# Two of three pairs of the layers' networks by seven block products, and modulation rows in the token mixings

## The chip, the cores and the metric

The kernel runs on one core of one Trainium2 chip, as one program. The metric is its device time in microseconds (us): the median of three runs of the kernel before was 2988.95 us (2986.76 to 2989.94). The engines are TensorE (PE, with its weight load PEld), VectorE (DVE), ScalarE (ACT), GpSimd (POOL) and SyncE (SP), whose queue issues nearly all transfers from device memory.

## The reference

A model of two blocks runs on one sequence of 512 tokens of width 1024. The first block has two layers, each a token mixing and a gated network with a convolution over the tokens; the second block has two swiglu networks with a bidirectional mLSTM and pooling mixer between them. All is float32. Vectors c, c_2 and c_ctx_2 are turned into modulation columns (shifts, scales and gates) by products with large matrices.

```
def first_block(x, c, ...):
    c_act = silu(c)
    for l in range(2):
        mod = (c_act @ ada_w[l] + ada_b[l])[:, None, :]           # 6 x 1024
        sh1, sc1, g1, sh2, sc2, g2 = split(mod, 6)
        h = rmsnorm(x, norm1_g[l]) * (1 + sc1) + sh1
        x = x + g1 * token_mix(h, w_in[l], w_fourier[l], w_ret[l], w_out[l])
        h = rmsnorm(x, norm2_g[l]) * (1 + sc2) + sh2
        x = x + g2 * conv_ffn(h, ffn_up[l], conv_w[l], conv_b[l], ffn_down[l])
    return rmsnorm(x, final_g)

def conv_ffn(h, w_up, conv_w, conv_b, w_down):                    # 1024 -> 2 x 2816 -> 1024
    u = h @ w_up
    up = pad(u, one token on each side)
    u = sum(up[:, i:i + S] * conv_w[i] for i in range(3)) + conv_b
    a, b = split(u, 2)
    return (gelu(a) * b) @ w_down

def second_block(x, c, ctx, c_ctx, w_mod, ...):
    mod  = (silu(c) @ w_mod + b_mod)                              # 9 x 1024, for x
    modc = (silu(c_ctx) @ w_mod + b_mod)                          # for the 256 context tokens
    # swiglu(x) and swiglu(ctx), mLSTM and pooling mixer, swiglu(x); each with ada_in, ada_out
```

token_mix projects h to seven parts, mixes one by a Fourier transform and three by chunked retention, merges the two results by sigmoid gates and projects them out.

## The kernel before

Activations lie with features on the 128 partitions and tokens along the columns. Every float32 operand is kept as a high and a low part, and a product is three matmuls: high by high, low by high, high by low (`mm`, lines 143 to 155). A weight block is loaded by `wload` (line 109): a transfer to one of four raw buffers, the high part by ACT (line 123), the low part by DVE (line 124). The network of a layer (`ffn`, line 383) runs over 22 pairs of 128 gate and 128 value columns. An ordinary pair is two weight blocks of 1024 × 128 times 512 tokens: 2 × 8 × 3 = 48 matmuls of 512 columns. Behind every group of five or six pairs stands a down projection. In the layers, the pair's two results go through the convolution (ACT line 854, DVE lines 855 and 857, each half), the gelu (ACT) and its product (DVE line 1054), and are split for the down projection (lines 140 and 141).

A pair can also be computed as a quad: its two 1024 × 128 blocks are seen as 2 × 2 blocks of 512, the activations as 2 × 2 blocks of 256 tokens by 512 features, and seven block products take the place of eight. `quad_w` (line 327) makes the sums and differences of weight blocks on DVE and splits them (lines 334 to 341); `combos` (line 302) makes four sums of activation blocks once per network, and splits them; `quad` (line 346) runs the seven products, 7 × 4 × 3 = 84 matmuls of 256 columns, and puts them together with ACT and DVE (lines 363 to 376). The kernel before does this in the networks of the second block, from pair 5 on.

The modulation columns are made by rows: a 512 KB load into a raw buffer and one multiplication with an accumulated sum on DVE (`modcols`, lines 259 to 272). They are a background: every `wload` adds a rate to a counter, and whenever the counter is over one the next row is issued. `drain_bg` issues what is left. In the first token mixing 32 rows are made so (rate 0.6), in the first network the 48 rows of layer 1 (0.8), in the second token mixing 32 rows of the second block (0.5), in the second network the other 40 blocks, each for two vectors (0.68). Which instruction stands behind which on an engine is fixed when the program is built, by a scheduler that starts from the program's order.

The profiled kernel's stages are: first token mixing to 545 us, first network to 925, second token mixing to 1420, second network to 1800, first swiglu network to 2320, mixer to 2607, last swiglu network from 2640 to the end.

Of the kernel before, what the change touches and what calls it, by code (L numbers as in the profile page):

```python
# [19 lines left out]
P = 128  # L20
D = 1024
KD = D // P
S = 512
# [19 lines left out]
    ("n1g", DEPTH * 8), ("n2g", DEPTH * 8), ("adab", DEPTH * 48), ("fing", 8),  # L43
    ("convw", DEPTH * 3 * 44), ("convb", DEPTH * 44),
    ("bmod", 72), ("npre", 24), ("npost", 24),
    ("convw2", 12), ("convb2", 4), ("pscale", 4), ("hnorm", 4),
]
COFF = {}
_o = 0
for _n, _c in COLS:  # L50
    COFF[_n] = _o
    _o += _c
NCOLS = _o


@with_exitstack
def tile_two_blocks(ctx: ExitStack, tc: tile.TileContext, I, out):
# [43 lines left out]
    def col(name, i):  # L101
        o = COFF[name] + i
        return cols[:, o:o + 1]

# [241 lines left out]
    def quad(w, B, tc_, n, mid=None):  # L346
# [10 lines left out]
        if 2 * n <= S:  # L357
            t, u2 = T(), T()[:, n:2 * n]
            s1, u3 = t[:, 0:n], t[:, n:2 * n]
        else:  # L360
            s1, u2, u3 = (T()[:, :n] for _ in range(3))
# [21 lines left out]
    def ffn(segs, up, down, groups, act_fn, sink, fp, bufs, heads, tails, hold=True,  # L383
# [59 lines left out]

        ready = {}

        def quad_prep(j):
            ready[j] = quad_w([up[j], up[NPAIR + j]])

        for at, (kind, gi, j) in enumerate(order):

            coming = None
            if seven and at + 1 < len(order) and order[at + 1][0] == "p" and order[at + 1][2] >= nh + 2:
                coming = lambda j=order[at + 1][2]: quad_prep(j)
            if kind == "p" and seven and nh <= j < nh + 2:
                seven["sums"](j - nh)
            if kind == "p" and seven and j == nh + 2 and "third" in seven:
                seven["third"]()
            if kind == "p" and seven and j >= nh + 2:
                hl, hid[j] = hid_slots(seven["last"] if j == NPAIR - 1 and "last" in seven else None)
                seven["fn"](*quad(ready.pop(j), seven["B"], seven["T"], seven["n"], coming), hl)  # L460
                if j == NPAIR - 1:
                    seven["end"]()
# [88 lines left out]
    ada = {i: ada_load(i) for i in (8, 0)}  # L551
    cols = cst.tile([P, NCOLS], F32, name="cols")
    sp.dma_start(cols, I["cols"])
    mods = []
# [6 lines left out]
    def mod1(l, idx, raws=None):  # L561
        modcols(I["adaT"][l], [(crow, mods[l][0], 48)], idx, raws)
# [11 lines left out]
    def token_mix(l, h, after, before_tail, ws, mo, mp, mid=None):  # L574
# [133 lines left out]
        with tc.tile_pool(name=f"fou{l}", bufs=1) as fp:  # L708
# [77 lines left out]
            seq(ps[:16], [[t.rearrange("p g k -> p (g k)") for t in asp[st]] for st in (0, 1)], tabs[0])  # L786
            Pt.append(split_bias(ps[:16], first[:16, 0:1], 16))

        with tc.tile_pool(name=f"mrg{l}", bufs=1) as gp:
# [70 lines left out]

    c2rows = []
    m2r = cst.tile([P, 2, 72], F32, name="m2r")
# [3 lines left out]

    def mod2(i):
        if not c2rows:
            c2rows.append(silu_row(I["c2"], crp))
        if i < 40 and len(c2rows) < 2:  # L870
            c2rows.append(silu_row(I["cc"], hq["pool"]))
        modcols(I["wmodT"], [(c2rows[0], m2r[:, 0, :], 72)] + ([(c2rows[1], m2r[:, 1, :], 40)] if i < 40 else []), [i])

# [124 lines left out]
    for l in range(DEPTH):  # L998
# [3 lines left out]
        if l == 0:  # L1002
            start0(mp)
            for i in range(16, 24):
                bgq.append(lambda i=i: mod1(0, [i]))
            bgq.append(lambda: fin1(0, 16, 24))
            for i in range(24, 48):
                bgq.append(lambda i=i: mod1(0, [i]))
            bgq.append(lambda: fin1(0, 24, 48))
            bgr[1] = 0.6  # L1010
        else:
            for i in range(40, 72):
                bgq.append(lambda i=i: mod2(i))
            bgr[1] = 0.5
        h = hq["h"]
# [16 lines left out]
        def start_ffn():  # L1032
            if l == 0:
                for i in range(48):
                    bgq.append(lambda i=i: mod1(1, [i]))
                bgq.append(lambda: fin1(1, 0, 48))
            else:
                for i in range(40):
                    bgq.append(lambda i=i: mod2(i))
            bgr[1] = 0.8 if l == 0 else 0.68  # L1040

        def before_ffn_tail():
            drain_bg(0.0)
# [12 lines left out]

        def sink1(si, m, ps, c, first):
# [14 lines left out]
        with tc.tile_pool(name=f"ffn{l}", bufs=1) as fp:  # L1072
            hq["pool"] = fp
# [23 lines left out]

    def swiglu_quad(pa, c12, c21, c22, hl):
        n = hl[0].shape[1] // 2
        one = 2 * n <= S  # L1100
        s_ = T() if one else None
        for i, (g, v) in enumerate(((pa, c21), (c12, c22))):
            t = s_[:, i * n:(i + 1) * n] if one else T()[:, :n]
            act.activation(t, g, AF.Sigmoid)
            dve.tensor_tensor(t, t, g, op=ALU.mult)
            if not one:
                dve.tensor_tensor(t, t, v, op=ALU.mult)
                split(t, *(a[:, i * n:(i + 1) * n] for a in hl))
        if one:
            dve.tensor_tensor(s_, s_, c21, op=ALU.mult)  # L1110
            split(s_, *hl)

# [51 lines left out]
    with tc.tile_pool(name="ffa", bufs=1) as fp:  # L1164
# [28 lines left out]
        def reload():  # L1193
            xc[:] = xc_load(xc_tile())
            x[:] = x_cols(x_tile())
            for k in range(KD):
# [6 lines left out]
            seven={"sums": sums, "third": lambda: third(B, Ts, N3), "B": B, "T": Ts, "n": N3,  # L1203
                   "fn": swiglu_quad, "end": lambda: None,
                   "last": [tz[:, i * T2:(i + 1) * T2] for i in (0, 1)]})
# [321 lines left out]
    with tc.tile_pool(name="ffb", bufs=1) as fp:  # L1527
        qs = ExitStack()
        qps = []

        def slot2():
            if not qps:
                qps.append(qs.enter_context(tc.tile_pool(name="qq", bufs=1, side="right")))
            return [qps[0].tile([P, 256], F32R, name=nm("tc")) for _ in (0, 1)]

        Ts2 = [[], [], [], []]
        B2 = [mcols(hlast[4 * i:4 * i + 4], c) for i in (0, 1) for c in HALVES]
        ffn([(S, hlast)], I["up2T"][1], I["down2T"][1], GROUPS3, swiglu, sink2([z]), fp, 8,
            (3, [(0, c) for c in HALVES]), [(0, c, finish) for c in HALVES], ws=headw,
            seven={"sums": lambda i: combos(B2, slot2, Ts2, (2 * i, 2 * i + 1), 256), "B": B2, "T": Ts2, "n": 256,  # L1540
                   "fn": swiglu_quad, "end": qs.close})

# [114 lines left out]
```

## Time and profile before

| | |
|---|---|
| median of three runs | 2988.95 us |
| the profiled run, its span | 2986.76 us, 2985.0 us |
| PE busy | 2919.9 us, 98% |
| DVE busy | 2115.3 us, 71% |
| ACT busy | 1155.5 us, 39% |
| mean rate of the transfers | 117 GB/s |
| mean granted PE clock | 0.990 |

The span goes from the first to the last instruction; the run's time is a little longer. Busy times are those of one profiled execution, and an engine can be busy without setting the end. [...] In a timeline a row is: start, duration, engine, line, operation, output and inputs, and in square brackets the idle time before it and what ended it. Where DVE or PE works back to back, the next instruction starts a little before the one ahead has ended, so a duration is longer than the distance to the next start. In a list of waits a row is: engine, its line, who released it, total us, times, longest.

### The profile page before, as it was taken

How to read it: one execution, taken by the hardware profiler on the slowest of the kernel's cores; microseconds unless marked ns; L12 is line 12 of the kernel's file. 1: busy time of each engine (PE TensorE's matmuls, PEld its weight loads, DVE VectorE, ACT ScalarE, POOL GpSimd, SP SyncE). 2: the span in 40 equal slices, each digit the busy share in tenths (PEclk: the TensorE clock that was granted, in tenths of full speed). 3: DMA queues.
4: the chain of work that ended last, by engine and by line, in shares of the span. 5: the costliest groups of instructions: out<-in, count | busy, mean ns of one | idle time of the engine just before them, and what ended most of it. 6: DMA issues, size and time to landing. Idle time of an engine off the chain costs nothing.

```text
span 2985.0 us, 42346 instructions
## 1 busy us (share of the span) xinstructions
PE 2919.9 (98%) x16612; PEld 2574.6 (86%) x16612; DVE 2115.3 (71%) x3756; ACT 1155.5 (39%) x1994; POOL 174.1 (6%) x121
## 2 busy tenths in 40 slices
PE   6999999999999999999999999999999999899998
PEld 4888888988889888888888899999999987789997
DVE  8766455777766665556888868677776677686786
ACT  4333333433343333334433345333233456444342
POOL 2000001000000000001000010000000180200001
PEclk9999999999999999999999999999999999999999
DMA  6444354266552333344355532122123220313331
GB/s 250 124 129 130 97 156 142 92 190 191 185 168 90 121 105 115 119 143 148 109 179 179 171 111 86 57 68 74 57 75 110 85 71 15 99 44 112 101 114 57
DMA packets 117560, 348.39 MB, mean 117 GB/s; under 512 B 12432, under 2 KB 26384, under 8 KB 117360
## 3 DMA queue, kind: packets, MB, share of 16 engines
q1 hardware_dynamic: 116208, 344.64, 36.6%
q8 instruction: 130, 2.13, 0.3%
q10 hardware_dynamic: 1152, 1.05, 0.1%
q14 instruction: 70, 0.57, 0.1%
HBM read 341.44 MB, written 4.19 MB: 116 GB/s over the span
## 4 chain that ended last, share of the span: by engine, by line
PE 93%; DVE 4%; ACT 1%; issue 0%; DMA 0%; POOL 0%; SPq 0%; DVEq 0%; ACTq 0%; POOLq 0%
PE mm L151 28%; PE mm L154 28%; PE mm L152 28%; PE sm L185 2%; PE mm L1454 1%; PE mm L626 1%; PE mm L628 1%; PE mm L627 1%; PE sm L193 1%; PE mm L1435 1%; PE mm L1249 0%; PE mm L1250 0%; DVE acc L225 0%; PE mm L1251 0%; DVE hl L242 0%
## 5 line engine op out<-in xcount | busy, mean ns | idle before, releaser
L123 ACT ACTIVATE whi<-raw 128x1024 fp32r<-128x1024 f32 (+3 forms) x467 | 449.8, 965 | 768.5 <-PE mm L152 500.5
L151 PE MATMUL mm<-hh,whi 128*128 128x512 f32 (+2 forms) x1988 | 730.4, 369 | 6.9 <-ACT hh L987 5.3
L152 PE MATMUL mm<-hl,whi 128*128 128x512 f32 (+2 forms) x1988 | 728.4, 367 | 2.5 <-DVE hl L242 2.2
L154 PE MATMUL mm<-hh,wlo 128*128 128x512 f32 (+2 forms) x1988 | 729.1, 367 | 1.4 <-POOL wlo L124 1.4
L124 DVE TENSOR_TENSOR wlo<-raw,whi 128x1024 fp32r<-128x1024 f32 (+4 forms) x450 | 499.0, 1115 | 248.6 <-ACT whi L123 244.3
L151 PEld LDWEIGHTS mm<-hh,whi 128*128 128x128 f32 x1988 | 376.2, 190 | 68.7 <-ACT hh L987 6.2
L152 PEld LDWEIGHTS mm<-hl,whi 128*128 128x128 f32 x1988 | 376.8, 190 | 61.9 <-DVE hl L242 3.0
L154 PEld LDWEIGHTS mm<-hh,wlo 128*128 128x128 f32 x1988 | 376.6, 190 | 59.1 <-POOL wlo L124 2.1
L151 PE MATMUL mm<-dh,whi 128*128 128x512 f32 (+1 forms) x760 | 275.0, 362 | 0.0
L152 PE MATMUL mm<-dh,whi 128*128 128x512 f32 (+1 forms) x760 | 268.4, 361 | 0.0
L154 PE MATMUL mm<-dh,wlo 128*128 128x512 f32 (+1 forms) x760 | 251.7, 362 | 0.0
L271 DVE SCALAR_TENSOR_TENSOR t<-ada,crow 128x1024 bf16<-128x1024 f32 x202 | 244.7, 1216 | 4.7 <-DMA ada<-adaT 4.7
L151 PEld LDWEIGHTS mm<-dh,whi 128*128 128x128 f32 x760 | 143.1, 188 | 29.3
L152 PEld LDWEIGHTS mm<-dh,whi 128*128 128x128 f32 x760 | 142.9, 188 | 23.2
L154 PEld LDWEIGHTS mm<-dh,wlo 128*128 128x128 f32 x760 | 133.1, 188 | 16.7
L124 POOL TENSOR_TENSOR wlo<-raw,whi 128x1024 fp32r<-128x1024 f32 x17 | 42.0, 2499 | 1760.8 <-ACT whi L123 1759.1
L855 DVE SCALAR_TENSOR_TENSOR t<-mm,cols,t 128x511 f32<-128x511 f32 (+1 forms) x96 | 70.6, 735 | 73.6 <-ACT t L854 73.2
L151 PE MATMUL mm<-tc,whi 128*128 128x256 f32 (+1 forms) x386 | 113.2, 295 | 0.0
L154 PE MATMUL mm<-tc,wlo 128*128 128x256 f32 (+1 forms) x386 | 112.4, 292 | 0.0
L152 PE MATMUL mm<-tc,whi 128*128 128x256 f32 (+1 forms) x368 | 106.6, 290 | 0.0
L1119 DVE TENSOR_TENSOR z<-z,mm 128x512 f32<-128x512 f32 (+1 forms) x112 | 67.3, 607 | 55.0 <-PE mm L154 54.6
L854 ACT ACTIVATE t<-mm,cols 128x512 f32<-128x512 f32 (+1 forms) x96 | 72.8, 759 | 70.8 <-PE mm L154 70.6
(478 smaller groups left out, 5871.8 us busy)
## 6 DMA issues: line engine op xcount, KB each, us to landing
ada<-adaT SPq DMA_DIRECT2D x96, 512.0 KB
raw<-winT SPq DMA_DIRECT2D x96, 512.0 KB
raw<-upT SPq DMA_DIRECT2D x88, 512.0 KB
raw<-up2T SPq DMA_DIRECT2D x88, 512.0 KB
ada<-wmodT SPq DMA_DIRECT2D x72, 512.0 KB
raw<-downT SPq DMA_DIRECT2D x32, 384.0 KB
raw<-down2T SPq DMA_DIRECT2D x22, 512.0 KB
raw<-downT SPq DMA_DIRECT2D x32, 320.0 KB
```

Of the source, the lines that this page charges most:

```text
L123: act.activation(hi[:p, :n], raw, AF.Copy)
L124: (eng or dve).tensor_tensor(lo[:p, :n], raw, f(hi[:p, :n]), op=ALU.subtract)
L151: pe.matmul(ps, lhsT=wh, rhs=r[k][0], start=first and k == 0, stop=False, skip_group_check=more)
L152: pe.matmul(ps, lhsT=wh, rhs=r[k][1], start=False, stop=False, skip_group_check=more)
L154: pe.matmul(ps, lhsT=wl, rhs=r[k][0], start=False, stop=last and k == n - 1, skip_group_check=more)
L185: pe.matmul(pm[:, t:t + 1], lhsT=sq[:, t * P:(t + 1) * P], rhs=meanc[:, mc:mc + 1], start=False, stop=i == len(parts) - 1 and t == nt - 1)
L193: pe.matmul(pr[:, t * P:(t + 1) * P], lhsT=y[:, t:t + 1].to_broadcast([P, P]), rhs=identL, start=True, stop=True)
L271: dve.scalar_tensor_tensor(junk, raw[:, :D], 1.0, vec, op0=ALU.mult, op1=ALU.mult, accum_out=dst[:, i:i + 1])
L626: pe.matmul(ps, lhsT=hh, rhs=wh, start=k == 0, stop=False)
L854: act.activation(t, ps, AF.Identity, bias=col(bname, bi), scale=col(wname, taps[1] + wi))
L855: dve.scalar_tensor_tensor(t[:, 1:n], ps[:, 0:n - 1], col(wname, taps[0] + wi), t[:, 1:n], op0=ALU.mult, op1=ALU.add)
L1119: dve.tensor_tensor(zz, zz, ps, op=ALU.add)
```

## The change

In the networks of the two layers, pairs 5, 6, 8, 9, 11, 12, 14, 15, 17, 18 and 20 become quads; the others from 3 on (3, 4, 7, 10, 13, 16, 19, 21) stay ordinary. The sums of activations are made at pairs 3 and 4. The convolution of a quad reads its results from SBUF; ACT copies one of its four blocks there. The frame for quads of 512 tokens becomes a helper, `seven512`, used in the layers and in the last network. The 48 rows of layer 1 move from the first network to the first token mixing (rate 1.28), and the rows of the second network to the second token mixing (rate 1.68), where the context's 40 rows load their blocks by themselves. The networks have no background of rows any more. The constants of the convolution (352 of 632 columns) are loaded at each layer network's start and no longer in the kernel's opening. The first swiglu network's quad function is separated from the last one's.

```
+NCOLS1 = COFF["convw"]
-        return cols[:, o:o + 1]
+        return cols[:, o:o + 1] if o < NCOLS1 else hq["ccols"][:, o - NCOLS1:o - NCOLS1 + 1]
...
+    def seven512(h, fn, **more):
+        qs = ExitStack()
+        qps = []
...
+        Ts = [[], [], [], []]
+        B = [mcols(h[4 * i:4 * i + 4], c) for i in (0, 1) for c in HALVES]
+        return {"sums": lambda i: combos(B, slot, Ts, (2 * i, 2 * i + 1), 256), "B": B, "T": Ts, "n": 256,
+                "fn": fn, "end": qs.close, **more}
...
+        nq = [j for j in range(nh + 2, NPAIR) if seven and seven.get("only", lambda j: True)(j)]
...
-            if kind == "p" and seven and j >= nh + 2:
+            if kind == "p" and j in nq:
...
-    def mod2(i):
...
+    def mod2(i, w_):
+        if w_ not in c2rows:
+            c2rows[w_] = silu_row(I["cc"], hq["pool"]) if w_ else silu_row(I["c2"], crp)
+        modcols(I["wmodT"], [(c2rows[w_], m2r[:, w_, :], 72)], [i])
...
-            bgr[1] = 0.6
+            for i in range(48):
+                bgq.append(lambda i=i: mod1(1, [i]))
+            bgq.append(lambda: fin1(1, 0, 48))
+            bgr[1] = 1.28
         else:
-            for i in range(40, 72):
-                bgq.append(lambda i=i: mod2(i))
-            bgr[1] = 0.5
...
+            for i in range(40):
+                bgq.append(lambda i=i: mod2(i, 1))
+            for i in range(72):
+                bgq.append(lambda i=i: mod2(i, 0))
+            bgr[1] = 1.68
...
         def start_ffn():
-            if l == 0:
-                for i in range(48):
-                    bgq.append(lambda i=i: mod1(1, [i]))
...
-            bgr[1] = 0.8 if l == 0 else 0.68
+            pass
...
+        def geglu_quad(j, hl, pa, v, t):
+            act.activation(v[:, 0:256], pa, AF.Copy)
+            split(geglu(v, t, j, S), *hl)
...
+            hq["ccols"] = fp.tile([P, NCOLS - NCOLS1], F32, name=nm("ccols"))
+            sp.dma_start(hq["ccols"], I["cols"][:, NCOLS1:])
...
-                      before_tail=before_ffn_tail, mid=mid, defer=True)
+                      before_tail=before_ffn_tail, mid=mid, defer=True,
+                      seven=seven512(h, geglu_quad, only=lambda j: j % 3 != 1 and j < NPAIR - 1))
```

On PE, in the first network, pair 4 (outputs mm_5270 and mm_5271 before) is followed by pair 5, which is ordinary before: weights whi/wlo times activations hh/hl of 512 columns.

```order
L154 MATMUL mm_5271<-hh_4612,wlo_5305 128x512
L151 MATMUL mm_5271<-hh_4614,whi_5304 128x512
L152 MATMUL mm_5271<-hl_4615,whi_5304 128x512
L154 MATMUL mm_5271<-hh_4614,wlo_5305 128x512
L151 MATMUL mm_5350<-hh_4600,whi_5354 128x512
L152 MATMUL mm_5350<-hl_4601,whi_5354 128x512
L154 MATMUL mm_5350<-hh_4600,wlo_5355 128x512
L151 MATMUL mm_5350<-hh_4602,whi_5354 128x512
L152 MATMUL mm_5350<-hl_4603,whi_5354 128x512
```

After the change pair 5's first product (mm_5687) is followed by five matmuls of a second one into the same output, and then by a product with sums of activations (tc) and of weight blocks (whi_5656). The row numbers of the source have moved by two.

```order
L153 MATMUL mm_5687<-hh_4801,whi_5650 128x256
L154 MATMUL mm_5687<-hl_4802,whi_5650 128x256
L156 MATMUL mm_5687<-hh_4801,wlo_5651 128x256
L184 LDWEIGHTS zero
L184 MATMUL sm_8551<-zero 128x2
L153 MATMUL mm_5687<-hh_4803,whi_5650 128x256
L154 MATMUL mm_5687<-hl_4804,whi_5650 128x256
L156 MATMUL mm_5687<-hh_4803,wlo_5651 128x256
L153 MATMUL mm_5687<-hh_4805,whi_5650 128x256
L154 MATMUL mm_5687<-hl_4806,whi_5650 128x256
L153 MATMUL mm_5688<-tc_5404,whi_5656 128x256
L154 MATMUL mm_5688<-tc_5405,whi_5656 128x256
```

The matmuls are half as wide, and the one into mm_5688 stands behind operands that DVE and ACT have to make first. On DVE, the opening of the same network has, before, the convolution's steps of pairs 0 to 3 (L855, L857), splits of weights (L124) and hidden results (L141), and modulation rows (L271) between them.

```order
L271 SCALAR_TENSOR_TENSOR t_5196,modr_120<-ada_5194,crow_94 128x1024
L141 TENSOR_TENSOR dh_5159<-t_5160,dh_5158 128x512
L855 SCALAR_TENSOR_TENSOR t_5178<-mm_4974,cols,t_5178 128x511
L271 SCALAR_TENSOR_TENSOR t_5230,modr_120<-ada_5228,crow_94 128x1024
L857 SCALAR_TENSOR_TENSOR t_5178<-mm_4974,cols,t_5178 128x511
L1054 TENSOR_TENSOR t_5174<-t_5174,t_5178 128x512
L124 TENSOR_TENSOR wlo_5355<-raw_5352,whi_5354 128x1024
L141 TENSOR_TENSOR dh_5173<-t_5174,dh_5172 128x512
L855 SCALAR_TENSOR_TENSOR t_5258<-mm_5186,cols,t_5258 128x511
L857 SCALAR_TENSOR_TENSOR t_5258<-mm_5186,cols,t_5258 128x511
L271 SCALAR_TENSOR_TENSOR t_5310,modr_120<-ada_5308,crow_94 128x1024
```

After the change DVE's rows end, at the same place before pair 5, with the last splits of sums (tc), the differences of pair 5's weight blocks (L336 to L343) and the two splits that make wlo_5657.

```order
L143 TENSOR_TENSOR tc_5567<-t_5556,tc_5566 128x256
L315 TENSOR_TENSOR t_5563<-t_5563,t_5561 128x256
L143 TENSOR_TENSOR tc_5571<-t_5561,tc_5570 128x256
L143 TENSOR_TENSOR tc_5575<-t_5554,tc_5574 128x256
L143 TENSOR_TENSOR tc_5579<-t_5563,tc_5578 128x256
L336 TENSOR_TENSOR t_5648<-raw_5645 128x512
L338 TENSOR_TENSOR raw_5645<-raw_5644,raw_5645 128x512
L878 SCALAR_TENSOR_TENSOR t_5673<-mm_5582,ccols_4947,t_5673 128x511
L339 TENSOR_TENSOR raw_5644<-t_5648,raw_5644 128x512
L143 TENSOR_TENSOR wlo_5657<-t_5648,whi_5656 128x512
L343 TENSOR_TENSOR raw_5644<-raw_5644 128x512
L143 TENSOR_TENSOR wlo_5657<-raw_5644,whi_5656 128x512
```

The modulation rows are gone from there, 48 instructions of 256 columns have come in before these rows, and wlo_5657 stands behind all of them. The third place is DVE in the output projection of the second token mixing; before, the sums into x (L834) stand among weight splits (L124) and splits of weight blocks that are held for later (L133).

```order
L834 SCALAR_TENSOR_TENSOR xb_99<-mm_11974,mod_121,xb_99 128x512
L133 TENSOR_TENSOR yrl_12083<-raw_12080,yrh_12082 128x512
L124 TENSOR_TENSOR wlo_12051<-raw_12048,whi_12050 128x512
L133 TENSOR_TENSOR yrl_12089<-raw_12086,yrh_12088 128x512
L834 SCALAR_TENSOR_TENSOR xb_99<-mm_11994,mod_121,xb_99 128x512
L133 TENSOR_TENSOR yrl_12095<-raw_12092,yrh_12094 128x512
L133 TENSOR_TENSOR yrl_12101<-raw_12098,yrh_12100 128x512
L133 TENSOR_TENSOR yrl_12107<-raw_12104,yrh_12106 128x512
L834 SCALAR_TENSOR_TENSOR xb_99<-mm_12014,mod_121,xb_99 128x512
```

After the change the modulation rows of the second block (L273) stand between the sums (now L857) and the weight splits (now L126).

```order
L857 SCALAR_TENSOR_TENSOR xb_99<-mm_13000,mod_121,xb_99 128x512
L126 TENSOR_TENSOR wlo_13045<-raw_13042,whi_13044 128x512
L143 TENSOR_TENSOR mgl_12987<-t_12901,mgh_12986 128x512
L273 SCALAR_TENSOR_TENSOR t_13050,m2r<-ada_13048,crow_10618 128x1024
L857 SCALAR_TENSOR_TENSOR xb_99<-mm_13028,mod_121,xb_99 128x512
L273 SCALAR_TENSOR_TENSOR t_13054,m2r<-ada_13052,crow_10618 128x1024
L126 TENSOR_TENSOR wlo_13073<-raw_13070,whi_13072 128x512
L857 SCALAR_TENSOR_TENSOR xb_99<-mm_13056,mod_121,xb_99 128x512
L273 SCALAR_TENSOR_TENSOR t_13078,m2r<-ada_13076,crow_10618 128x1024
L273 SCALAR_TENSOR_TENSOR t_13082,m2r<-ada_13080,crow_10618 128x1024
L857 SCALAR_TENSOR_TENSOR xb_99<-mm_13084,mod_121,xb_99 128x512
L126 TENSOR_TENSOR wlo_13101<-raw_13098,whi_13100 128x512
```

The splits of L133 have moved behind, and a row of 1024 columns stands ahead of nearly every sum and split.

## Rows read from the trace of the kernel before

**Rows 1.** The page: span, busy time of each engine, the chain's shares by engine.
```profile
span 2985.0 us, 42346 instructions
...
PE 2919.9 (98%) x16612; PEld 2574.6 (86%) x16612; DVE 2115.3 (71%) x3756; ACT 1155.5 (39%) x1994; POOL 174.1 (6%) x121
...
PE 93%; DVE 4%; ACT 1%; issue 0%; DMA 0%; POOL 0%; SPq 0%; DVEq 0%; ACTq 0%; POOLq 0%
```

**Rows 2.** Windows: length, busy (count) of PE, PEld, DVE, ACT, POOL; clock; DMA share; GB/s.
```profile
557.00:905.00 348.00, 348.00 (x1715) 293.39 (x1714) 249.00 (x359) 134.12 (x176) 0.00 (x0) 1.00 0.54 171
1436.00:1785.00 349.00, 349.00 (x1701) 294.37 (x1700) 282.39 (x438) 134.17 (x181) 9.52 (x4) 0.99 0.51 157
936.00:1145.00 209.00, 209.00 (x1120) 179.48 (x1119) 136.90 (x232) 75.58 (x131) 0.00 (x0) 1.00 0.37 116
1215.00:1420.00 205.00, 203.88 (x1077) 173.72 (x1076) 122.59 (x198) 71.22 (x119) 14.23 (x8) 1.00 0.45 141
```

**Rows 3.** Waits of PE, 1420 to 1800 and 2660 to 2930: total, times, longest.
```profile
PE mm L152 <- DVE hl L242: 0.8, 1, 0.8
PE mm L151 <- ACT t L363: 0.5, 1, 0.5
```

**Rows 4.** Windows of five ordinary pairs and of six quads.
```profile
648.86:703.85 54.99, 54.99 (x240) 44.97 (x239) 37.10 (x51) 21.09 (x28) 0.00 (x0) 1.00 0.49 147
2736.02:2795.80 59.78, 59.78 (x506) 59.34 (x505) 55.72 (x99) 31.93 (x52) 0.00 (x0) 1.00 0.30 102
```

**Rows 5.** Timeline of DVE, last network's opening: start, duration, instruction.
```profile
2669.32 0.42 DVE L141 TENSOR_TENSOR tc<-t,tc 128x256 fp32r<-128x256 f32 x1
...
2669.99 1.09 DVE L141 TENSOR_TENSOR tc<-t,tc 128x256 fp32r<-128x256 f32 x3
...
2671.60 0.68 DVE L1094 TENSOR_TENSOR t<-t,mm 128x512 f32<-128x512 f32 x1
2672.20 0.68 DVE L336 TENSOR_TENSOR raw<-raw,raw 128x512 f32<-128x512 f32 x1
```

**Rows 6.** Window of the last network's opening, 73 DVE instructions.
```profile
2640.40:2675.80 35.40, 34.87 (x205) 30.48 (x204) 34.44 (x73) 19.07 (x35) 0.00 (x0) 1.00 0.19 60
```

**Rows 7.** Timelines of DVE and, last, ACT, opening of the first layer's network.
```profile
564.05 1.22 DVE L124 TENSOR_TENSOR wlo<-raw,whi 128x1024 fp32r<-128x1024 f32 x1 [6.32 <-ACT whi L123]
565.19 0.74 DVE L855 SCALAR_TENSOR_TENSOR t<-mm,cols,t 128x511 f32<-128x511 f32 x1
565.97 0.75 DVE L857 SCALAR_TENSOR_TENSOR t<-mm,cols,t 128x511 f32<-128x511 f32 x1
...
575.83 0.74 DVE L857 SCALAR_TENSOR_TENSOR t<-mm,cols,t 128x511 f32<-128x511 f32 x1
576.49 0.74 DVE L855 SCALAR_TENSOR_TENSOR t<-mm,cols,t 128x511 f32<-128x511 f32 x1
...
578.41 1.21 DVE L271 SCALAR_TENSOR_TENSOR t<-ada,crow 128x1024 bf16<-128x1024 f32 x1
...
579.55 0.68 DVE L141 TENSOR_TENSOR dh<-t,dh 128x512 fp32r<-128x512 f32 x1
...
599.37 0.78 ACT L854 ACTIVATE t<-mm,cols 128x512 f32<-128x512 f32 x1 [2.51 <-PE mm L154]
```

**Rows 8.** Window at the kernel's start; waits of SP's queue for modulation rows.
```profile
8.00:18.00 10.00, 2.41 (x10) 2.33 (x11) 7.92 (x22) 4.77 (x7) 0.00 (x0) 1.00 1.03 399
...
SPq L266 <- DVE t L271: 111.9, 45, 5.0
```

**Rows 9.** Timeline of PE at the second block's start; the window behind it.
```profile
1829.64 0.39 PE L151 MATMUL mm<-ch,whi 128*128 128x256 f32 x1 [2.57 <-DVE t L1094]
...
1830.40:1833.80 3.40, 3.40 (x18) 3.40 (x18) 3.40 (x7) 1.57 (x3) 0.00 (x0) 0.50 0.66 252
```

**Rows 10.** Timeline of DVE, second token mixing's output projection.
```profile
1371.19 0.75 DVE L834 SCALAR_TENSOR_TENSOR xb<-mm,mod,xb 128x512 f32<-128x512 f32 x1 [0.85 <-PE mm L154]
...
1379.55 0.75 DVE L834 SCALAR_TENSOR_TENSOR xb<-mm,mod,xb 128x512 f32<-128x512 f32 x1 [0.23 <-PE mm L154]
```

More of the change, by code (lines that the diff above doesn't have):

```diff
@@ L376, in quad, with pool, slot @@
         dve.tensor_tensor(u2, u2, pc, op=ALU.add)
-        return pa, u2, t if 2 * n <= S else s1, u3
+        return (pa, v, t) if 2 * n <= S else (pa, u2, s1, u3)
+    def seven512(h, fn, **more):
+        qs = ExitStack()
+        qps = []
+        def pool():
+            if not qps:
+                qps.append(qs.enter_context(tc.tile_pool(name=nm("qp"), bufs=1, side="right")))
+            return qps[0]
+        def slot():
+            return [pool().tile([P, 256], F32R, name=nm("tc")) for _ in (0, 1)]
+        Ts = [[], [], [], []]
+        B = [mcols(h[4 * i:4 * i + 4], c) for i in (0, 1) for c in HALVES]
+        return {"sums": lambda i: combos(B, slot, Ts, (2 * i, 2 * i + 1), 256), "B": B, "T": Ts, "n": 256,
+                "fn": fn, "end": qs.close, **more}
     def head_ws(up, nh):
@@ L451, in ffn @@
             coming = None
-            if seven and at + 1 < len(order) and order[at + 1][0] == "p" and order[at + 1][2] >= nh + 2:
+            if seven and at + 1 < len(order) and order[at + 1][0] == "p" and order[at + 1][2] in nq:
                 coming = lambda j=order[at + 1][2]: quad_prep(j)
@@ L551, in tile_two_blocks @@
     ada = {i: ada_load(i) for i in (8, 0)}
-    cols = cst.tile([P, NCOLS], F32, name="cols")
-    sp.dma_start(cols, I["cols"])
+    cols = cst.tile([P, NCOLS1], F32, name="cols")
+    sp.dma_start(cols, I["cols"][:, :NCOLS1])
     mods = []
@@ L787, in token_mix @@
             Pt.append(split_bias(ps[:16], first[:16, 0:1], 16))
+        if l == 1:
+            ccs.close()
         with tc.tile_pool(name=f"mrg{l}", bufs=1) as gp:
@@ L859, in conv @@
         return t
-    c2rows = []
+    c2rows = {}
     m2r = cst.tile([P, 2, 72], F32, name="m2r")
@@ L1096, in swiglu, with swiglu_quad3, swiglu_quad @@
         return s_
[L1098 to L1101, printed above, removed]
+    def swiglu_quad3(j, hl, pa, c12, c21, c22):
+        n = N3
         for i, (g, v) in enumerate(((pa, c21), (c12, c22))):
-            t = s_[:, i * n:(i + 1) * n] if one else T()[:, :n]
+            t = T()[:, :n]
             act.activation(t, g, AF.Sigmoid)
             dve.tensor_tensor(t, t, g, op=ALU.mult)
[L1106 to L1111, printed above, removed]
+            dve.tensor_tensor(t, t, v, op=ALU.mult)
+            split(t, *(a[:, i * n:(i + 1) * n] for a in hl))
+    def swiglu_quad(j, hl, pa, v, t):
+        s_ = T()
+        for g, c in ((pa, HALVES[0]), (v[:, 256:512], HALVES[1])):
+            act.activation(s_[:, c[0]:c[1]], g, AF.Sigmoid)
+            dve.tensor_tensor(s_[:, c[0]:c[1]], s_[:, c[0]:c[1]], g, op=ALU.mult)
+        dve.tensor_tensor(s_, s_, t, op=ALU.mult)
+        split(s_, *hl)
     def sink2(zs):
@@ L1527, in tile_two_blocks @@
     with tc.tile_pool(name="ffb", bufs=1) as fp:
[L1528 to L1537, printed above, removed]
         ffn([(S, hlast)], I["up2T"][1], I["down2T"][1], GROUPS3, swiglu, sink2([z]), fp, 8,
             (3, [(0, c) for c in HALVES]), [(0, c, finish) for c in HALVES], ws=headw,
-            seven={"sums": lambda i: combos(B2, slot2, Ts2, (2 * i, 2 * i + 1), 256), "B": B2, "T": Ts2, "n": 256,
-                   "fn": swiglu_quad, "end": qs.close})
+            seven=seven512(hlast, swiglu_quad))
 def _consts():
```

25 lines of the change are left out of this document (8 added, 17 removed).

## The prediction

> **What bounds the kernel now.** I read the page's totals and the chain of waits first. PE is busy for 98% of the span and 93% of the chain that ended last is PE's own work [rows 1]. So a saving counts where PE has fewer columns to stream, and a cost counts where PE is made to wait. Next come the stages [rows 2]: in both layer networks (557 to 905 and 1436 to 1785 us) PE is busy throughout, while DVE works 249 and 282 of some 348 us. PE's waits in and around these stages are tenths of a microsecond [rows 3]. There is no PE idle time to win, and DVE has 19 to 28% to give. Last, I read the last swiglu network (2660 to 2930), which already runs its pairs as quads, because the change makes the layer networks resemble it.
>
> **The gain.** Five ordinary pairs, 240 matmuls of 512 columns, take 54.99 us, 11.00 a pair; six quads of the last network, 504 matmuls of 256 columns (and two small ones), take 59.78 us, 9.96 a quad [rows 4]. The change turns 11 pairs in each layer into quads: 22 × 1.04 = 22.8 us less PE work.
>
> **The opening of each network, where the quads are paid for.** Pair 5 is the first quad, and before its second product DVE must have made 48 instructions of sums and splits of 256 columns (in pairs 3 and 4) and the block differences of pair 5's weights. Prices are from start to start where DVE works back to back [rows 5, 7]: 0.335 for 256 columns, 0.60 for 512, 1.14 for 1024, 0.66 to 0.78 for a convolution step (0.70 taken). From pair 3's first weights (564.05 in the trace) to the split that releases the second product, DVE now has 84 instructions: 5 × 1.14 + 17 × 0.70 + 14 × 0.60 + 48 × 0.335 = 42.1 us. The last network's opening shows how far such a sum holds: its 73 instructions (33.8 us by the same prices, with 20 of 512 columns and none of the convolution) took 35.4 us [rows 6]. With its 1.6 us of gaps the layer opening takes 43.7 us and ends at 607.75.
>
> PE is done with pair 4 at 599.3, where ACT's convolution step had waited for it [rows 7], and has 21 matmuls of pair 5 (at 59.78/504 = 0.119 us) that it may do first: 601.8. It waits 6.0 us. In the trace the same spot of the last network cost 0.5 us [rows 3], since there DVE had no convolution to do. Behind the released product, 26 more DVE instructions (3 × 1.14 + 10 × 0.60 + 7 × 0.70 + 6 × 0.335 = 16.3 us) stand before the sum that pair 6's sixth product waits for; PE fills 111 × 0.119 + 4 × 0.23 = 14.1 us of it. That makes 2.2 more: 8.2 us a layer, 16.4 for both. With no gaps and a wait of only 1 us at pair 6 it would be 5.3 a layer; with every instruction at its whole duration (0.42, 0.68, 0.75, 1.22 in rows 5 and 7) DVE's 84 take 48.5 us and the opening costs 13.0. I take 8.2, since start-to-start distances are what consecutive instructions of this kernel show.
>
> [...]
>
> **After the opening.** A quad asks of DVE two 1024-column and seven 512-column instructions for weights, five of 256 to combine products, four convolution steps and two more of 512: 2 × 1.14 + 9 × 0.60 + 5 × 0.335 + 4 × 0.70 = 12.2 us against PE's 9.96. An ordinary pair asks 6.3 against 11.0. Two quads and one pair make 30.7 us on DVE and 30.9 on PE: level, with the down projections between them as slack. In six quads of the last network DVE was busy 55.72 of 59.78 us with no PE wait [rows 4]. Over the first layer's stage DVE goes from 249 to about 249 − 48 × 1.14 (modulation rows gone) + 11 × 5.9 + 17 = 276 of 337 us. I put no wait here; with the opening's debt not worked off, it would be 2.2 us at a quad that follows a quad. New on ACT are one 256-column copy per quad and the weights' halves; ACT works 134 of 348 us there [rows 2], so nothing.
>
> **The modulation rows.** One is a 512 KB load and one DVE instruction of 1024 columns; behind it the next instruction starts 1.14 us later [rows 7]. 48 go from the first network to the first token mixing; 40 × 2 go from the second network to the second mixing, where the two vectors now load the same 40 blocks separately (+21 MB). In the second mixing, retention (936 to 1145) goes from 137 to about 177 us of DVE in 209 (35 rows more by the order), the merge (1215 to 1420) from 123 to 166 in 205 (38 more) [rows 2]: covered on average, not everywhere. In the output projection DVE now has 13 rows among its own work, 13 × 1.14 + 10 × 0.60 + 8 × 0.66 = 26.1 us, where PE needs 8 columns × 2.80 (from 1371.19 to 1379.55 in three steps [rows 10]) = 22.4; the queue's tail is overtaken by what follows, so I book 2 us. For all other places where a row stands ahead of a weight split I book 2 more: 4.0 in all. Bounds: −1 (the networks' own DVE queue gets shorter) to +15, a tenth of the 128 × 1.14 = 146 us moved. The loads: the second mixing goes from 116 to 141 GB/s [rows 2] by 80 × 0.524 MB over 484 us = 87, to some 205 to 230, where the trace has 399 in a full stretch [rows 8]. A row keeps one of four raw buffers until DVE has read it, and SP's loads of rows already wait 111.9 us for earlier rows to be read [rows 8]. They will wait longer, with the weight loads queued behind them; PE feels this only where DVE is late anyway, and it is in the 4.0.
>
> **Clock.** A PE wait of 2.57 us at 1829.64 is followed by 18 matmuls at a granted clock of 0.50, the lower level, from 1830.40 on [rows 9]; they take 3.4 us in place of about 2.1. The two waits at the openings are longer, so I book 1 us each, 2.0. [...]
>
> **Smaller edits.** The convolution's constants are loaded at each network's start, long before the first convolution: nothing. The opening load shrinks by 180 KB: 0.4 us at 399 GB/s [rows 8]. The second block's first network runs the same steps under another name: nothing.
>
> **Sum.** The profiled run took 2986.8 us (its span 2985.0 [rows 1]): 2986.8 − 22.8 − 0.4 + 16.4 + 4.0 + 2.0 = 2986.0. The median of the runs shown is 2.2 above the profiled one, so the median should be 2988.
>
> **Rivals.** *A: the opening is hidden.* If DVE finds its new work done in gaps (it idled 6.32 us just before 564.05 [rows 7], and the modulation rows that stood between are gone), each opening costs 2 us as the last network's cost little, the mixings 2 and the clock nothing: 2986.8 − 23.2 + 4 + 2 = 2969.6, or 2971.8 as a median. Against it: DVE's order puts the sums behind pair 3's convolutions, which wait for PE. *B: DVE falls behind and stays behind.* It decides if the 84 instructions take over 46 us. Openings at 13.0 (+9.6) and 2.2 us at every second of the eight later quads that follow a quad (+8.8): 3006.6, slower. For it: quads and pairs level at 30.7 to 30.9. Against it: rows 4. *C: the modulation rows surface in the mixings* at a tenth of their time, +14.6: 3002.8. For it: 80 to 85% DVE in two stages; against it: those stages' PE waits are now under 2 us in 209 and 205 [rows 2]. That PE's gain isn't there is excluded by rows 4.
>
> **Chances.** Forecast 0.42 (its own range 2982 to 2994), A 0.28, B 0.18, C 0.12. Within 0.2%, some 6 us, a measurement of this kernel can't be told from no change: 2983 to 2995. Faster: nearly all of A and a fifth of the forecast, 0.36; same: most of the forecast, 0.32; slower: B, C and a little of the forecast, 0.32. The range 2968 to 3005 leaves out the best part of A and half of B.
>
> **What would show it.** Right: quads of about 9.96 us on PE in both networks; a PE wait of 5 to 7 us at pair 5 on ACT or DVE and a second of about 2 at pair 6; a stretch of granted clock 0.50 behind the first; PE waits in the second mixing's output projection. Wrong: waits under 1 us at pair 5 (A), waits at pairs 9, 12 and 15 (B), PE idle for over 5 us in either mixing (C).

## The result, and the profile after

The changed kernel takes 3007.61 us (median of four runs, 3000.71 to 3012.3) against 2988.69 before: a ratio of 1.0062, 95% interval 1.0044 to 1.0079. It is slower by 18.9 us, where no change was forecast, and above the range. The profiled run is the longest of the four, 3012.3 us, 25.5 above the profiled run of before.

The page's span, busy times and chain of the kernel after answer to [rows 1]:

```profile
span 3010.5 us, 44696 instructions
...
PE 2921.0 (97%) x17404; PEld 2608.4 (87%) x17404; DVE 2288.8 (76%) x4116; ACT 1217.6 (40%) x2134; POOL 176.0 (6%) x121
...
PE 50%; DVE 7%; DMA 3%; ACT 2%; issue 1%; POOL 0%; DVEq 0%; ACTq 0%; POOLq 0%
```

PE is as busy as before although it has less to stream; its mean granted clock is 0.982, 0.990 before, so some of its matmuls ran at a lower one (0.56 over 27 of them, below). The chain now passes through transfers (3%) and DVE (7%). Next are the stages that answer to [rows 2], in the same order and columns (the ends are moved with the work; the clock is a share of the full one):

```profile
568.00:916.00 348.00, 341.49 (x2113) 305.29 (x2112) 275.02 (x440) 164.13 (x245) 0.00 (x0) 0.99 0.32 99
1466.00:1812.00 346.00, 339.39 (x2092) 303.55 (x2091) 275.50 (x444) 165.58 (x252) 10.47 (x4) 0.99 0.32 98
947.00:1159.00 212.00, 209.52 (x1116) 180.34 (x1115) 172.37 (x300) 72.74 (x129) 0.00 (x0) 0.99 0.59 190
1233.00:1448.00 215.00, 207.24 (x1075) 174.47 (x1073) 168.11 (x276) 73.00 (x119) 13.92 (x8) 0.99 0.72 227
```

DVE's load was forecast well: 275 us in the first network (276), 172 and 168 in the two stretches of the second mixing (177 and 166). What the time shows is not in these sums. Two marks place it: ACT's first convolution step of each layer network, timeline of the kernel after (at 563.92 and 1439.57 before; DVE took the first up at 565.19 [rows 7]):

```profile
574.87 0.76 ACT L877 ACTIVATE t<-mm,ccols 128x512 f32<-128x512 f32 x1
...
1469.58 0.76 ACT L877 ACTIVATE t<-mm,ccols 128x512 f32<-128x512 f32 x1
```

By them and three more such marks, this is how much later the same instruction starts than in the profiled run of before (the difference of two trace times, one profiled execution each). The profiled runs of the kernel after, of the first quad at 8 and of the same at rate 1.6 are 4.7, 4.5 and 8.6 us above the medians of their kernels; the others lie within 3.5 us of theirs:

```
                                network 1   mixing 2   its output    network 2   second
                                starts      starts     projection    starts      block
before (us)                       563.92     931.90     1371.19       1439.57    1829.50
after                              +11.0      +10.9       +21.1         +30.0      +26.8
rows only (no quads)                +5.7       +5.6       +13.9         +23.8      +23.0
quads only (rows as before)         -1.0      +18.5       +16.1         +15.5      +71.3
rows issued faster                  +1.5       +1.6       +24.1         +23.8      +21.4
first quad at 8                     +9.1       +3.0        +9.3         +16.9       +7.5
first quad at 8, rate 1.6           +1.5       -3.1        +6.6         +15.0       +6.8
the same, 48 rows to networks       +2.0       +3.8        +3.7          +3.4       +3.0
after without loads                 +5.6       +4.9        +4.2          +8.6       +5.4
after with short rows               +6.0       +6.0        +7.3         +13.7      +11.0
first quad at 8, paired loads       +2.5       -1.7        +2.1          +1.8       -8.9
the same, all quads from 8          +0.9      +10.2       +19.4         +19.1      +25.6
the same, no quads                  +1.5       +1.5        +9.9          +9.6       +6.1
the same, quads from 5              +1.2       +3.4        +7.6          +7.2       +4.3
```

Both mixings lose: 11.0 us up to the first network, 19.1 through the second mixing. Rows with the same code up to a mark tell how far one execution can be trusted. Five of them have the first mixing of the kernel after and stand between +5.6 and +11.0 at the first network; the seven with the faster rate there stand between +0.9 and +2.5. Through the second mixing, the four with 112 loads at rate 1.68 lose 13.9 to 19.1 us, and the four with paired loads 3.5 to 8.9. The two networks, with all their quads, come out at -0.1 and -3.2: the openings eat what the quads give. PE's waits in the kernel after (engine, line, releaser: total, times, longest), at the first mixing's end (480 to 560), at the first opening (575 to 640) and at the second mixing's end (1380 to 1480):

```profile
PE sm L187 <- DVE acc L227: 4.1, 2, 3.5
...
PE mm L153 <- ACT t L365: 3.5, 1, 3.5
...
PE mm L153 <- ACT whi L125: 2.8, 2, 2.0
PE mm L156 <- DVE wlo L126: 2.3, 2, 1.1
```

Timelines of DVE and PE at that opening, and the window behind PE's wait:

```profile
575.00 1.23 DVE L126 TENSOR_TENSOR wlo<-raw,whi 128x1024 fp32r<-128x1024 f32 x1 [6.50 <-ACT whi L125]
...
617.36 0.69 DVE L143 TENSOR_TENSOR wlo<-raw,whi 128x512 fp32r<-128x512 f32 x1
...
615.28 0.58 PE L153 MATMUL mm<-hh,whi 128*128 128x256 f32 x1 [3.49 <-ACT t L365]
```

```profile
615.30:621.30 6.00, 5.76 (x27) 5.46 (x28) 6.00 (x10) 2.73 (x4) 0.00 (x0) 0.56 0.15 40
```

DVE's 84 instructions take from 575.00 to 618.05: 43.0 us, with 43.7 forecast. PE stands for 3.5 us, until ACT's copy of the first product is made, which stands behind splits that DVE had to feed first, and then 27 matmuls run at a granted clock of 0.56 on average, in 5.8 us for 3.2 at 0.119.

In the second mixing (950 to 1425) ACT, which makes the high parts of all weights, shows what changed. First two rows of its waits after, then its first row before (950 to 1405):

```profile
ACT whi L125 <- DMA raw<-winT: 69.7, 29, 7.8
ACT whi L125 <- DMA raw<-wretT: 31.8, 7, 4.8
```

```profile
ACT whi L123 <- PE mm L152: 96.4, 30, 4.8
```

Before, ACT was ahead of PE and waited for PE to free a weight. After, it waits for weights to land: the lead is gone, and PE is exposed to late loads. One cause stands in the waits of SP's queue in the second mixing (950 to 1420, before and after): the issue of a weight load waits for the DVE instruction of the row whose buffer it needs.

```profile
SPq L111 <- DVE t L271: 19.6, 15, 2.5
```

```profile
SPq L113 <- DVE t L273: 76.3, 47, 8.0
```

### The profile page after: what moved, and what is told of

Its sections match the earlier page's. It is cut to its first block, busy times and chain, and to the rows that moved or that the text cites. A ratio compares the mean times of both kernels' runs of the same rounds, so it can differ in the third digit from the quotient of the medians.

```text
span 3010.5 us, 44696 instructions
## 1 busy us (share of the span) xinstructions
PE 2921.0 (97%) x17404; PEld 2608.4 (87%) x17404; DVE 2288.8 (76%) x4116; ACT 1217.6 (40%) x2134; POOL 176.0 (6%) x121
## 4 chain that ended last, share of the span: by engine, by line
PE 50%; DVE 7%; DMA 3%; ACT 2%; issue 1%; POOL 0%; DVEq 0%; ACTq 0%; POOLq 0%
PE mm L153 15%; PE mm L156 15%; PE mm L154 15%; PE mm L1482 1%; PE sm L187 1%; DMA ada<-wmodT 1%; DVE t L273 1%; DVE wlo L126 1%; ACT whi L125 1%; DMA rwf<-wf 1%; PE mm L1463 1%; DVE acc L227 1%; DMA raw<-winT 0%; DMA raw<-woutT 0%; PE mm L1277 0%
## 5 line engine op out<-in xcount | busy, mean ns | idle before, releaser
L126 DVE TENSOR_TENSOR wlo<-raw,whi 128x1024 fp32r<-128x1024 f32 (+4 forms) x472 | 515.0, 1095 | 254.5 <-ACT whi L125 249.3
L153 PE MATMUL mm<-hh,whi 128*128 128x512 f32 (+2 forms) x1900 | 669.3, 354 | 15.7 <-ACT t L365 8.1
L154 PE MATMUL mm<-hl,whi 128*128 128x512 f32 (+2 forms) x1900 | 666.9, 352 | 6.3 <-DVE hl L1009 4.2
L156 PE MATMUL mm<-hh,wlo 128*128 128x512 f32 (+2 forms) x1900 | 665.7, 351 | 0.3 <-DVE wlo L126 0.3
L153 PEld LDWEIGHTS mm<-hh,whi 128*128 128x128 f32 x1900 | 361.1, 191 | 64.0 <-ACT t L365 9.3
L156 PEld LDWEIGHTS mm<-hh,wlo 128*128 128x128 f32 x1900 | 361.7, 191 | 42.7 <-DVE wlo L126 0.7
L273 DVE SCALAR_TENSOR_TENSOR t<-ada,crow 128x1024 bf16<-128x1024 f32 x202 | 242.8, 1220 | 10.8 <-DMA ada<-wmodT 7.2
L153 PE MATMUL mm<-tc,whi 128*128 128x256 f32 (+1 forms) x738 | 215.0, 292 | 2.1 <-ACT whi L142 1.6
L156 PE MATMUL mm<-tc,wlo 128*128 128x256 f32 (+1 forms) x738 | 211.2, 287 | 0.0
L154 PE MATMUL mm<-tc,whi 128*128 128x256 f32 (+1 forms) x720 | 206.4, 287 | 0.0
L126 POOL TENSOR_TENSOR wlo<-raw,whi 128x1024 fp32r<-128x1024 f32 x17 | 42.5, 2516 | 1808.9 <-ACT whi L125 939.5
L153 PEld LDWEIGHTS mm<-tc,whi 128*128 128x128 f32 x738 | 140.1, 190 | 8.5 <-DVE t L370 2.8
L156 PEld LDWEIGHTS mm<-tc,wlo 128*128 128x128 f32 x738 | 140.1, 190 | 0.0
L154 PEld LDWEIGHTS mm<-tc,whi 128*128 128x128 f32 x720 | 136.9, 190 | 0.3
```

What stands on the lines that cost most here:

```text
L126: (eng or dve).tensor_tensor(lo[:p, :n], raw, f(hi[:p, :n]), op=ALU.subtract)
L153: pe.matmul(ps, lhsT=wh, rhs=r[k][0], start=first and k == 0, stop=False, skip_group_check=more)
L154: pe.matmul(ps, lhsT=wh, rhs=r[k][1], start=False, stop=False, skip_group_check=more)
L156: pe.matmul(ps, lhsT=wl, rhs=r[k][0], start=False, stop=last and k == n - 1, skip_group_check=more)
L273: dve.scalar_tensor_tensor(junk, raw[:, :D], 1.0, vec, op0=ALU.mult, op1=ALU.mult, accum_out=dst[:, i:i + 1])
```

## The experiments

Theory R: the rows in the mixings cost the time, through DVE (D1) or through the loads and the four raw buffers (D2). Rival Q: the quads cost it, by an opening debt (O) or at each quad that follows a quad (B).

**Rows only.**

```
-                      seven=seven512(h, geglu_quad, only=lambda j: j % 3 != 1 and j < NPAIR - 1))
+                      )
```

> The changed kernel with ordinary pairs only in the layers: the modulation rows stay in the token mixings, no quads there. Theory R (the rows in the mixings cost the time, the quads come out even): 2988.7 + 20 = about 3009, with the loss at the ends of the two mixings. Rival Q (the quads' openings and clock cost it, the rows are covered): 2988 to 2992.

3003.37 us, ratio 1.0053 (1.0038 to 1.0068). The rows alone cost 14.9 us. By the table they cost it in the two mixings, in the second about half of it (8.3 of 18.2) ahead of the output projection. Q as the only cause falls; the quads on top cost another 4.

**Quads only.** The rows' code of before is put back, with its rates and its `drain_bg` behind each network.

```
-            bgr[1] = 1.28
+            bgr[1] = 0.6
...
-            bgr[1] = 1.68
+            bgr[1] = 0.5
...
         def start_ffn():
-            pass
+            if l == 0:
+                for i in range(48):
+                    bgq.append(lambda i=i: mod1(1, [i]))
...
+            bgr[1] = 0.8 if l == 0 else 0.68
```

> The quads of the changed kernel with the modulation rows where they were before (48 and 40 blocks in the networks). Theory R with DVE short in the networks: the mixings lose nothing, but DVE has 276 + 55 = 331 us of work in 337 in the first network and about 282 + 82 = 364 in the second, so 27 us or more are lost there: about 3010 to 3020. If the quads come out even in spite of the rows: 2985 to 2990. Rival Q: over 3005 with waits of PE at the two openings alone.

3057.29 us, 1.0236 (1.0221 to 1.0251), far over both. PE's longest wait in its second network:

```profile
PE mm L153 <- DVE xb L1082: 28.3, 1, 28.3
```

A quad's weights don't pass through `wload` and so don't pull rows: the 13 blocks left over in the second network (26 instructions of 1.14 us, 29.6) were issued together by `drain_bg` at its end, and PE stood behind them for 28.3 us. That is about half of the 55.8 us that this network loses; the first network loses 19.5, and where the rest is lost was not traced. The mixings lose nothing without the added rows (-1.0, and -3.0 through the second), as theory R has it. So moving the rows out was needed with this counter, and the number says little on DVE's capacity.

**Rows issued faster.**

```
-            bgr[1] = 1.28
+            bgr[1] = 1.6
...
-            bgr[1] = 1.68
+            bgr[1] = 2.1
```

> The changed kernel with the rows issued faster (rates 1.6 and 2.1 for 1.28 and 1.68), so that the last row is issued 11 to 13 weight loads before the end of its mixing. Theory R in its narrow form (a row ahead of the held weights and of the next network's first weights makes them late, and PE stands at the mixing's end): 9 and 10 us are won at the two ends, some 3 given back before: about 2992. Rival (the sum of DVE work and loads in the mixing counts, wherever it stands): 3005 to 3012, no change.

3009.66 us, 1.0075 (1.0058 to 1.0092): no change in the sum, but the table splits it. The first mixing's loss is gone (+1.5 for +11.0 at the first network); there 80 rows fit if none stands ahead of the held weights and the next network's first ones. The second mixing lost nothing at its end and all of it earlier, +22.5 before the output projection: 112 rows don't fit, early (here) or late (before). The time is the rival's; the narrow form holds for the first mixing only.

**First quad at pair 8.**

```
-only=lambda j: j % 3 != 1 and j < NPAIR - 1
+only=lambda j: j % 3 != 1 and 8 <= j < NPAIR - 1
```

> The changed kernel with pairs 5 and 6 ordinary: the first quad is pair 8, nine quads a layer. Theory O (an opening debt of DVE of about 8 us a layer, which three ordinary pairs in a row pay off): openings -16 to -18 us, their clock -3, two quads less a layer +4.2: about 2991. Rival (DVE stays behind whenever a quad follows a quad): the waits move to pairs 8 and 9, 3005 to 3010.

2992.54 us, 1.0018 (1.0009 to 1.0027): 15.1 less than after. PE's waits in its first network (575 to 920):

```profile
PE mm L153 <- ACT dh L142: 1.6, 1, 1.6
PE mm L153 <- ACT t L365: 0.5, 1, 0.5
```

The 3.5 us at the opening did not move to pair 8. Theory O holds, and a quad that follows a quad makes PE wait 0.5 us at most here (the 1.6 is a hidden result that a down projection waits for).

**Both repairs; 48 rows of the second mixing in the networks.**

```
-            for i in range(72):
+            for i in range(24):
...
-            bgr[1] = 1.68
+            bgr[1] = 1.25
...
+            if j == 8:
+                for i in range(24 + 24 * l, 24 + 24 * (l + 1)):
+                    bgq.append(lambda i=i: mod2(i, 0))
+                bgr[1] = 1
```

> First quad at pair 8 (as in the run before) and the first mixing's rows at rate 1.6; the second mixing stays at 1.68. The run with rates 1.6 and 2.1 lost nothing at the first mixing's end (its profile is 1.5 us behind the kernel before at the first network, where the changed kernel is 10.9 behind). If the two repairs add up: 2992.5 - 8 = about 2984.5. If the first mixing's loss only comes back later: 2992.

> The same with 48 of the second block's 112 rows taken out of the second mixing: 24 into each layer network from pair 8 on (rate 1.0), 64 left in the mixing (rate 1.25). Theory D (a mixing pays for every row above what its DVE or its loads can hold; the networks with nine quads have room for 24): the second mixing's loss goes from some 19 to some 5, the networks pay 2 to 4: about 2973. Rival (the networks pay for rows as they did with all of them, 3057): 2990 or more.

2989.44 (1.0006, 0.9994 to 1.0017) and 2990.19 us (0.9999, 0.999 to 1.0009). The first repair added 3 us of the 8 to the median. The table shows 7.6 at the first network and a second mixing that loses 18.1 for 13.9, but these are two single executions, the second of them 8.6 us above its median, and the code of that mixing is the same; why the median gained so little stays open. With 64 rows the second mixing's loss is gone (+3.8 to +3.4), and the networks give it back: from +2.0 to +3.8 and +3.4 to +3.0, where the run without their rows gains 4.6 and 8.2. The networks pay some 14 us for 2 to 4 expected, and the time is the rival's: the price moved.

**Loads or DVE.** The two halves of a row's cost, taken out one at a time in the second mixing.

```
-        modcols(I["wmodT"], [(c2rows[w_], m2r[:, w_, :], 72)], [i])
+        modcols(I["wmodT"], [(c2rows[w_], m2r[:, w_, :], 72)], [i], raws=[c2rows[w_]])
...
```

The instruction's factor is 0.001 instead of 1.0 here.

> The changed kernel without the loads of the second block's 112 rows: each row's DVE instruction multiplies the vector with itself (so the modulation of the second block isn't computed), DVE's work is the same. Theory D1 (DVE's time is what the second mixing lacks): no change, 3003 to 3010. Theory D2 (the loads and the raw buffers that they hold make the weights late): the second mixing's 19 us shrink to some 4: about 2993.

```
+        modcols(I["wmodT"], [(c2rows[w_], m2r[:, w_, :], 72)], [i], n=64)
...
```

> The changed kernel with all loads, but each of the 112 rows of the second block is multiplied over 64 of its 1024 columns only (the modulation isn't computed in full); DVE is spared about 112 x 0.95 us. Theory D1: about 2993 or less. Theory D2: 3003 to 3010.

2992.92 (1.0017, 1.0008 to 1.0027) and 2998.82 us (1.0033, 1.0021 to 1.0045). The first is D2's time, the second lies between the two forecasts. Through the second mixing the profiles lose 3.7 us without loads and 7.7 with short rows; with both parts it is 19.1, and 13.9 at the least. So each alone is mostly hidden, the loads are the larger part, and together they cost more than their sum. ACT's largest wait for weights (950 to 1425), without loads and with short rows:

```profile
ACT whi L125 <- PE mm L154: 129.2, 45, 5.4
```

```profile
ACT whi L125 <- DMA raw<-winT: 62.9, 24, 6.5
```

Without loads ACT is ahead of PE again; with short rows it still waits for landings.

**One load for two vectors**, on the run of 2989.44 us:

```
+        for w_ in ((0, 1) if i < 40 else (0,)):
...
+        modcols(I["wmodT"], [(c2rows[0], m2r[:, 0, :], 72)] + ([(c2rows[1], m2r[:, 1, :], 40)] if i < 40 else []), [i])
...
-            for i in range(40):
-                bgq.append(lambda i=i: mod2(i, 1))
...
-            bgr[1] = 1.68
+            bgr[1] = 1.25
```

> First quad at pair 8 and the first mixing's rows at 1.6 (as two runs before), and in the second mixing one load for the 40 blocks that two vectors need, as in the kernel before: 72 loads of rows for 112, at rate 1.25, with the same 112 DVE instructions. Theory D2 (four raw buffers, each held for the 4 to 5 us of a load and until DVE has read it, are what the second mixing lacks): its loss of 18 us falls to some 5, as without loads (4), so 2989.4 - 12 = about 2978, faster than both. Theory D1 (DVE's time): 2987 to 2990, no change.

2977.87 us, 0.9969 (0.9958 to 0.998): faster than both kernels, and what D2 said. It differs from the run of 2989.44 by the 40 loads fewer and by their issue; DVE's 112 instructions are the same. Through the second mixing it loses 3.5 us for 18.1 (by the medians 11.6 less). Its rows also end ahead of the output projection (the last at 1354.8, the first sum into x at 1373.2), while there the last row came at 1396.5, behind the first sum at 1377.8. That place alone isn't it: with rates 1.6 and 2.1 the rows ended at 1346.0, ahead of the projection at 1395.3, and 22 us were lost all the same.

With every pair from 8 to 20 a quad:

```
-only=lambda j: j % 3 != 1 and 8 <= j < NPAIR - 1
+only=lambda j: 8 <= j < NPAIR - 1
```

> The same with every pair from 8 to 20 a quad, 13 a layer for 9, so 8.3 us less PE work. If DVE's total decides (by starts 189 us of DVE from pair 8 on against 200 of PE, the down projections included): about 2971. Theory B (a quad asks 12.2 us of DVE against 9.96 of PE, and without an ordinary pair between them each quad makes PE wait up to 2.2 us): 13 quads in two layers lose up to 40 us between down projections, 2985 to 3010.

3012.18 us, 1.0084 (1.0071 to 1.0097). Theory B is right here. PE's waits in its first network (570 to 960):

```profile
PE mm L153 <- ACT t L365: 10.4, 7, 1.5
PE mm L156 <- DVE wlo L126: 4.6, 7, 0.7
```

Seven quads wait, some 2 us each. A quad's 12.2 us of DVE against 9.96 of PE can be borne for two quads between ordinary pairs, not for a long row of them.

The last two runs take the quads out, or put them back to pair 5:

```
-                      seven=seven512(h, geglu_quad, only=lambda j: j % 3 != 1 and 8 <= j < NPAIR - 1))
+                      )
...
-only=lambda j: j % 3 != 1 and 8 <= j < NPAIR - 1
+only=lambda j: j % 3 != 1 and j < NPAIR - 1
```

> The kernel of 2977.9 (rows at rate 1.6 in the first mixing, 72 loads at rate 1.25 in the second) with ordinary pairs only. If the mixings hold their rows now (its profile is 1.8 us behind at the second network, with 4 us gained by quads in the first): rows alone cost 2 to 6 us, 2990 to 2994, and the 18 quads are worth 13 to 16. If part of its gain comes from the networks without rows rather than from quads: below 2988.

> The kernel of 2977.9 with quads from pair 5 on as in the changed kernel, 11 a layer. The opening's debt alone, with the mixings mended: 2 x (8.2 + 1 to 2 of clock) more and 4.2 less: about 2992. Rival (the opening cost that much only because the mixing ahead left DVE and the loads late): 2974 to 2978.

2991.48 (1.0015, 1.0005 to 1.0024) and 2991.12 us (1.0013, 1.0003 to 1.0022). The rows, mended, still cost 3.5 us over the runs of before beside them (2987.97), and 18 quads are worth 13.6, 0.76 each, whatever the first of them costs included. Quads from 5 cost 13.3 more than quads from 8 although they are four more: the opening has its price without any late mixing, and PE's wait there is the one of the kernel after:

```profile
PE mm L153 <- ACT t L365: 3.5, 1, 3.5
```

## Why the prediction was wrong

- **The step that failed is the 4.0 us for the modulation rows.** They cost 14.9 us alone, with +11.0 and +19.1 in the changed kernel's profile. The step priced a row as 1.14 us of DVE, found DVE at 80 to 85%, and settled the loads in a clause: "PE feels this only where DVE is late anyway". The runs did not bear that out: without the loads the median falls by 14.7 us, with DVE spared by 8.8. A load holds one of four raw buffers while it lands, 4.3 us in the median (row below), and until DVE has read it; with 112 of them in the second mixing for 32, the issue of weight loads waited for rows' buffers (76.3 us for 19.6), ACT lost its lead, and late weights reached PE. The rate that I set against 399 GB/s, 205 to 230, was about right (190 and 227 in the two stretches). That it is hardly the limit is my estimate, not shown: at a mean of 208 GB/s a row's load landed in 4.3 us, and at 215, in the run with short rows, in 4.3 too (950 to 1420). That the four buffers are the limit is argued from these waits; no run gave the rows more buffers or a queue of their own.

The list of transfers of the kernel after, second mixing (950 to 1420): issues, KB each, median us to landing:

```profile
ada<-wmodT SPq DMA_DIRECT2D x109, 512.0 KB, 4.3
```

- **Its bounds were too low.** +15 at the most came from a tenth of DVE's time; the rows alone reached it, and the sum below books 20.0. Rival C, from the same tenth, named the place, and its sign came: PE is busy for 207.24 of the 215 us from 1233 on, so it idles 7.8. C's 3002.8 is 4.8 us short, and its chance of 0.12 was too small. Rival B's 3006.6 is nearer by luck alone: behind the first network's opening the longest wait of PE for a quad is 0.5 us, where B had 2.2 at every second quad that follows a quad.
- **The first mixing** was priced as if only the second were crowded. Its 5 last rows stood among the output projection, and the first weights of the network came late (last section); at rate 1.6 its 80 rows cost 1.5 us.
- **DVE's work at the opening was right:** 43.0 us for 43.7. The opening's price was booked as 18.4 us for two with the clock; the last runs give 13.3 + 4 × 0.76 = 16.3, and the marks of the kernel after 2 × 11 × 0.76 - 0.1 - 3.2 = 13.4. The parts differ. PE did 12 matmuls of pair 5 ahead of its wait, not 21, since the rest stand behind ACT's copy. It waited 3.5 us, not 6.0, since that copy came before the last split was made, and the 2.2 at pair 6 did not come (0.3 at most). The 27 matmuls behind the wait took 2.6 us longer at a granted clock of 0.56, while DVE finished its splits; what is left of the 6.7 to 8.2 us a layer was not traced. The bound of 13.0, at whole durations, was not reached: DVE's starts were as close as in [rows 5], 0.33 to 0.34 us apart for 256 columns and 0.60 for 512 where it worked back to back (593.36 to 595.04 and 616.16 to 617.96).
- **Quads** are worth 0.76 us each, less than the 1.04 taken from undisturbed stretches; where the rest goes was not tried. That the two-of-three pattern brings hardly a wait at the second of two quads was right, and that it is near its limit too: with every pair a quad, seven of them wait.
- **The 18.9 us split by the runs:** openings +16.3, rows in the mixings +20.0 (16.5 between the last run and the kernel after, and the 3.5 that remain), quads -22 × 0.76 = -16.7: +19.6. The terms are differences of the same medians and add up by construction, so this shares the loss out and doesn't confirm it; by the run with rows only, the rows' share is 14.9.

## What to carry to other kernels

Work moved under another stage has as many prices as the resources it holds there: here a row is 1.14 us of DVE, but also a buffer for the landing time (4.3 us) and the wait behind it. Count loads against buffers, landing time and the wait for the reader, not only busy shares and GB/s, and look at who waits for whom: an engine that goes from waiting for its consumer to waiting for its loads, as ACT did here (96.4 us for PE before, 69.7 for transfers after), has lost the lead that hid other delays. And a transform that saves on the bound engine by adding to its feeder should start where the feeder has a margin: three pairs later, with one load for two uses, the change gained 0.3% (2977.87 us against 2987.36).

## What the runs showed of the hardware

DVE's adds of 256 columns into acc took up to six times their time next to GpSimd's weight splits: of the twelve that the next norm waits for in the two kernels, the six that overlap a split took 1.60 to 2.59 us, the other six 0.42 or 0.43. Timelines of DVE and POOL at the first mixing's end, kernel after:

```profile
525.73 5.12 DVE L227 TENSOR_TENSOR acc<-acc,t 128x256 f32<-128x256 f32 x2 [1.63 <-ACT t L218]
...
531.73 0.42 DVE L227 TENSOR_TENSOR acc<-acc,t 128x256 f32<-128x256 f32 x1 [0.48 <-ACT t L218]
```

```profile
525.47 2.41 POOL L126 TENSOR_TENSOR wlo<-raw,whi 128x1024 fp32r<-128x1024 f32 x1 [472.14 <-ACT whi L125]
528.17 2.40 POOL L126 TENSOR_TENSOR wlo<-raw,whi 128x1024 fp32r<-128x1024 f32 x1 [0.30 <-DVE acc L227]
```

Two adds that overlap the two splits took 5.12 us together (2.43 and 2.59); the next, between splits, 0.42. Why the overlap makes them longer the traces don't show. This bears on the first mixing's end. Before, the splits began 12 us earlier, at 513.63, and two of the sums that the next norm waits for met them (1.88 and 1.67 us); after, four did, and took 7.3 us longer than at 0.42 each, for 2.7 before. The difference of 4.6 us can be a part of what this end lost; no run moved the splits alone.
